# Two projection tiles computed as a fifth seven-product pair instead of singly, with one tile instead of two kept for the end of the input projection

## The chip, the cores and the metric

The kernel runs on one core of one Trainium2 chip. The metric is device time in microseconds (us) of that core; lower is better. The profile names five engines: PE (TensorE, with PEld for its weight loads), DVE (VectorE), ACT (ScalarE), POOL (GpSimd) and SP (SyncE, which here issues nearly all DMAs).

## The reference

One decoder layer over 1024 tokens with model width 1024, all in float32:

```python
u = rms_norm(x, norm1_g)
z = u @ w_in                      # 1024 x 3584: 28 tiles of 128 columns
y_conv = group_rms_norm(cb * causal_dwconv3(cc * ch, conv_w), conv_norm_g, 8)
o = chunkwise_retention(rotary(q), rotary(k), v)          # 4 heads x 128
y_ret = group_rms_norm(o, ret_norm_g, 4) * silu(rg)       # rg: tiles 20 to 23
x = x + concat(y_conv, y_ret) @ w_out
x = x + relu(rms_norm(x, norm2_g) @ w_up)**2 @ w_down
out = rms_norm(x, final_norm_g)
```

What matters here is the end of `u @ w_in`: its last tiles are the gates `rg`, one tile per retention head (tile 20 + h gates head h), and what follows, `concat(y_conv, y_ret) @ w_out`, which needs all eight tiles of y (four of the convolution, y0 to y3, and four of the heads, y4 to y7).

## The kernel before, in words

Everything is kept transposed: 128 channels by 1024 tokens make a tile, and the tokens are split into two halves of 512. Float32 products are done in three matmuls: each operand is split into a rounded high part and the rest (`wh` and `wl` for weights, `uh`/`ul`, `yh`/`yl` or the two halves of `U` for activations), and high times high, high times low and low times high are accumulated in a PSUM bank of 128 x 512 (`b`). A split is a cast on ACT and a subtraction on DVE or POOL. So one tile of the input projection over one half of the tokens is 8 blocks of 128 channels times 3 = 24 matmuls.

The tiles of the input projection are computed in one of three ways.

- `whole(f)` (L744, through `tile_in`, L520): one tile over both halves, 48 matmuls in four slots of 12. The results are read from PSUM by DVE.
- `pair_in((f, g))` (L824): two tiles at once by a Strassen-like scheme: seven products of 12 matmuls (`product`, L779) in the place of eight. It needs sums of the inputs (`U`, the four entries t1 to t4, 16 units of on-chip memory of 128 x 1024), sums of the weight blocks (four POOL subtractions or additions in `Left.split`, L209), seven weight splits, and DVE additions that put the products together in on-chip memory. The products come in the order `UP_ORDER`; of the second tile, half 1 is finished with product 7 and half 0 with product 4.
- the end (L910 to L926): the tiles of `IN_END` over half 0, then over half 1, each step 12 matmuls.

Before, the turns are 0, 1, 2, 3, 20, the pairs (4, 5), (6, 7), (8, 9), (10, 11), then tile 21 whole, then 22 and 23 by halves at the end: four slots for tile 21 and eight for the end.

On-chip memory is full at this place, so y0, y1 and the outputs of heads 2 and 3 are spilt to DRAM (`put_by`, L867) and fetched back (`get_back`, L876) on SP's queue. SP's queue also fetches the weight pieces (`r`, four buffers): a piece's DMA waits there until its buffer is free, and everything issued after it waits behind it. The split weights have four buffers too, so ACT can run at most four pieces ahead of PE.

After the end the first matrix of the next stage, `group(0)` (L1060), starts at once on PE: its first step multiplies the first `w_out` piece with half 0 of y0, y1, y2 and y3 in this order (`yh`, `yl`).

Between PE's products the kernel places the work of the other engines with a small planner: each conv, gate, norm or split is a generator, and `background` (L428) chooses, by a cost table of its own, which engine gets the next step and where in the program it stands. The program is static: each engine runs its list in order. `done` and `norm` (L471) are the group norm of a conv tile: a square on ACT, two matmuls on PE (L483, L484), a reciprocal root on ACT and three operations on DVE. `gate` (L719) multiplies with the token norm `R`, applies Silu on ACT and multiplies with the head's output on DVE. The reciprocal root and Silu each need a table load on ACT when they alternate.

Of the kernel before, what the change touches and what calls it, by code (L numbers as in the profile page):

```python
# [36 lines left out]


IN_QK = [12, 13, 16, 17, 14, 15, 18, 19]
IN_TURNS = [0, 1, 2, 3, 20, (4, 5), (6, 7), (8, 9), (10, 11), 21]  # L40
IN_END = [22, 23]
SLOT, LOOK, PE_MARGIN, LATE = 2.72, 3.2, 1.2, 0.0
WARM = 10
NORM_MARGIN, STEP_MARGIN, POOL_LATE = 6.5, 0.3, 1.0
# [35 lines left out]
def hybrid_layer(  # L80
# [18 lines left out]
    now, clock, procs, got = [0.0], {}, [], {}  # L99
# [24 lines left out]
    def unit(dt=F32, s="u"):  # L124
        return big.tile([P, T], dt, tag="u", name=nm(s))
# [6 lines left out]
    def bank(pool_=None):  # L132
        return (pool_ or pm).tile([P, H], F32, tag="b", name=nm("b"))
# [54 lines left out]
    IN_ORDER = list(IN_QK)  # L188
    for turn in IN_TURNS + IN_END:
        IN_ORDER += turn if isinstance(turn, tuple) else [turn]  # L190
# [37 lines left out]
    ahead = 3  # L228
    for turn in IN_TURNS + IN_END:
        if isinstance(turn, tuple):  # L230
            o = Left(mix, 1)
# [190 lines left out]
    def spawn(gen, ready=None, late=0.0):  # L422
        Task(gen, now[0] if ready is None else ready, late).go()
# [4 lines left out]
    def background(look=LOOK):  # L428
        while True:
            best = None  # L430
            for task in list(procs):
                want = task.want
                if want is None or isinstance(want, float):
                    if task.ready + (want or PE_MARGIN) <= now[0] or look > 1e6:
                        best = (-1.0, task, None)
                        break
                elif isinstance(want, tuple) and isinstance(want[0], Engine):
                    for eng in want:
                        start = max(clock[eng], task.ready)
                        if start < now[0] + look:  # L440
                            end = start + eng.cost(H) + task.late
                            if best is None or end < best[0]:
                                best = (end, task, eng)
                elif want in got:
                    best = (-1.0, task, got[want])
                    break
            if best is None:
                return
            _, task, eng = best
            if isinstance(eng, float):  # L450
                task.ready = max(task.ready, eng)
                task.go()
            elif eng is None:
                task.go()
            else:
                clock[eng] = max(clock[eng], task.ready)
                task.go(eng)
                task.ready = max(task.ready, clock[eng])
# [4 lines left out]
    def force(key):  # L463
        while key not in got:
            background(1e9)
            assert key in got, key

    y, y_h, y_l = [None] * KT, [None] * KT, [None] * KT
# [108 lines left out]
    o_n, retention_task = {}, [None, None]  # L577
# [166 lines left out]
    def whole(f):  # L744
        def evac(z):
            if f < 20 and f % 3 == 0:
                out = a_of[f // 3] = unit(s="a")
                for half, sl in enumerate(hs):
                    act.copy(out[:, sl], z[half])
                return  # L750
            out = None if f < 20 and f % 3 == 1 else unit(s="z")
            for half in range(2):
                spawn(use(f, half, out, z[half], True), clock[dve])

        tile_in(evac)
# [12 lines left out]
    U = {}  # L768
# [55 lines left out]
    def pair_in(fs):  # L824
        out = [unit(s="z") for _ in range(2)]
        (c11, c12), (acc, c22) = ([o[:, sl] for sl in hs] for o in out)
        for at, n in enumerate(UP_ORDER):
            if not got.get("pairs") and n in (5, 6, 7, 4):
                for j in range(4):
                    force(({5: "t1", 6: "t2", 7: "t3", 4: "t4"}[n], j))  # L830
            b = product(n, (pm, pr)[at % 2])
            slot()
            prepare()
            ready = None
            if n == 1:
                act.copy(acc, b)
            if n == 2:
                dve.tensor_add(c11, acc, b)
                ready = 0, 0
            if n == 5:  # L840
                b5 = b
            if n in (6, 7, 4):
                dve.tensor_add(acc, acc, b)
            if n == 6:
                dve.tensor_add(c12, acc, b5)
            if n == 7:
                dve.tensor_add(c22, acc, b5)
                ready = 1, 1
            if n == 3:
                dve.tensor_add(c12, c12, b)  # L850
                ready = 0, 1
            if n == 4:
                ready = 1, 0
            if ready:
                f, half, o = fs[ready[0]], ready[1], out[ready[0]]
                if f < 20 and f % 3 == 0:
                    a_of[f // 3] = o
                else:
                    spawn(use(f, half, o, o[:, hs[half]], False), clock[dve], LATE * half)
            tick()  # L860
        got["pairs"] = now[0]
# [5 lines left out]
    def put_by(key, of, *ready):  # L867
        for r in ready:
            yield r
        yield (dve,)  # L870
        t = of()
        spilt[key] = spill.tile([P, T], F32, tag="sp", name=nm("sp"))
        nc.sync.dma_start(spilt[key], t)
        mark(("by", key), dve)

    def get_back(key):  # L876
        t = unit(s="back")
        nc.sync.dma_start(t, spilt.pop(key))
        return t

    def split_y(idx, half):
        yield "y", idx, half
        if idx < 2:
            yield "back", idx
        yield (act,)
        split_y_hi(idx, half)
        eng = yield (pool, dve)
        split_y_lo(idx, half, eng)
        mark(("split", idx, half), eng)
# [3 lines left out]
    for i in range(2):  # L893
        spawn(put_by(("y", i), lambda i=i: y[i], ("y", i, 0), ("y", i, 1)))
    for at, turn in enumerate(IN_TURNS):
        if isinstance(turn, tuple):
            pair_in(turn)
        else:
            whole(turn)
        if at == len(IN_TURNS) - 2:  # L900
            for h in (2, 3):
                force(("by", ("o", h)))
                o_n[h, 0] = o_n[h, 1] = get_back(("o", h))
            for i in range(2):
                force(("by", ("y", i)))
                y[i] = get_back(("y", i))
                got["back", i] = now[0] + 10.0
    for idx in range(KT):
        spawn(split_y(idx, 0))
    ends = {f: (unit(s="z"), [bank() for _ in hs], []) for f in IN_END}  # L910
    for half in range(2):
# [547 lines left out]
    o = unit(s="end")  # L1459
# [104 lines left out]
```

## Time and profile before

| quantity | value |
|---|---|
| median of 3 runs | 1070.92 us (1070.82 to 1071.99) |
| the profiled execution's own time | 1070.03 us |
| its span, first to last instruction | 1068.1 us |
| time around the span | 1.93 us |
| PE busy | 1054.8 us (99% of the span) |
| DVE busy | 870.8 us (82%) |
| POOL busy | 561.6 us (53%) |
| ACT busy | 463.6 us (43%) |
| PE's granted clock | 0.999 of full speed |

How to read it: the profile is of one execution, whose own time lies 0.89 us below the median. In a timeline or a group of lines, a row names the engine, the line of the kernel, the operation, the tile written and the tiles read, with the shapes; "idle before" is the time the engine stood still ahead of it and what it then waited for. Nearly all operations outside PE are issued through one helper and carry its line, L74, so they are told apart by the names of their tiles: `wh`, `wl` weight splits; `yh`, `yl` splits of y; `r` weight pieces or the small tiles of a norm; `z` results of projection tiles; `cv` a convolution; `back` a tile fetched back; `q` the output of a head.

### The profile page before, as it was taken

The page shows a single profiled execution, that of the slowest core. Times are in us where ns is not written, and L with a number is a line of the kernel's source. Part 1 is how long each engine was busy: PE and PEld are TensorE (multiplying, and loading weights), DVE is VectorE, ACT ScalarE, POOL GpSimd, SP SyncE. Part 2 cuts the span into 40 slices and gives each one's busy share as a digit, 9 for nine tenths or more (in the row PEclk, how much of TensorE's full clock was granted, in tenths as well). Part 3 has the DMA queues.
Part 4 walks back from the last instruction along what each step waited for, and adds up shares of the span by engine and source line. Part 5 has one row for each costly group of instructions (what it writes and reads, how often), then busy time and mean ns, then how long its engine had stood idle before and what let it go on. Part 6 is the DMA issues. An engine that isn't in the chain of part 4 may idle for free.

```text
span 1068.1 us, 13853 instructions
## 1 busy us (share of the span) xinstructions
PE 1054.8 (99%) x4860; PEld 879.2 (82%) x4860; DVE 870.8 (82%) x1231; ACT 463.6 (43%) x906; POOL 561.6 (53%) x381
## 2 busy tenths in 40 slices
PE   9999999999999999999999999999999999999997
PEld 8888888788888888788788888888888888888886
DVE  7446546799998665799999989999899899899955
ACT  8211445673437444443343433343443434334453
POOL 6334324367854233559458267277186295384552
PEclk9999999999999999999999999999999999999999
DMA  7121122122223733051221211211301201200204
GB/s 276 65 58 42 38 80 70 63 95 80 69 69 129 256 115 123 11 187 39 61 59 49 79 31 50 90 30 50 99 21 50 89 21 49 90 21 19 69 30 158
DMA packets 39685, 82.25 MB, mean 77 GB/s; under 512 B 4544, under 2 KB 5696, under 8 KB 39616
## 3 DMA queue, kind: packets, MB, share of 16 engines
q1 hardware_dynamic: 39328, 80.85, 23.5%
q8 instruction: 38, 0.62, 0.2%
q10 hardware_dynamic: 288, 0.52, 0.1%
q14 instruction: 31, 0.25, 0.1%
HBM read 71.92 MB, written 9.44 MB: 76 GB/s over the span
## 4 chain that ended last, share of the span: by engine, by line
PE 90%; DVE 6%; ACT 2%; issue 1%; POOL 1%; DVEq 0%; ACTq 0%; POOLq 0%
PE b L403 55%; PE b L1277 23%; PE b L357 4%; PE b L1386 4%; DVE t L74 1%; DVE wl L74 1%; DVE x L74 1%; DVE m L74 1%; ACT h L74 1%; DVE q L74 1%; DVE V L74 1%; PE b L339 0%; PE b L595 0%; PE b L1436 0%; PE b L246 0%
## 5 line engine op out<-in xcount | busy, mean ns | idle before, releaser
L74 ACT CAST wh<-r 128x512 fp32r<-128x512 f32 x286 | 176.6, 620 | 326.4 <-PE b L403 134.4
L403 PE MATMUL b<-U,wh 128*128 128x512 f32 x1024 | 315.8, 390 | 2.0 <-DVE x L74 1.2
L74 DVE TENSOR_TENSOR wl<-r,wh 128x512 fp32r<-128x512 f32 x250 | 232.8, 933 | 89.0 <-ACT wh L74 87.8
L74 POOL TENSOR_TENSOR r<-r,r 128x512 f32<-128x512 f32 x136 | 210.2, 1548 | 114.1 <-DVE wl L74 66.1
L1277 PE MATMUL b<-V,wh 128*128 128x512 f32 x784 | 242.0, 389 | 0.7 <-POOL V L74 0.4
L403 PEld LDWEIGHTS b<-U,wh 128*128 128x128 f32 x1024 | 191.7, 188 | 43.2 <-issue 2.4
L74 DVE TENSOR_TENSOR x<-x,b 128x512 f32<-128x512 f32 (+1 forms) x312 | 195.5, 673 | 28.8 <-PE b L1386 14.3
L403 PE MATMUL b<-U,wl 128*128 128x512 f32 x512 | 199.2, 389 | 0.0
L1277 PEld LDWEIGHTS b<-V,wh 128*128 128x128 f32 x784 | 147.1, 188 | 32.4 <-POOL V L74 0.9
L74 POOL TENSOR_TENSOR t<-t,t 128x512 f32<-128x512 f32 x70 | 106.3, 1523 | 96.4 <-ACT t L74 50.4
L1277 PE MATMUL b<-V,wl 128*128 128x512 f32 x392 | 152.5, 389 | 0.0
L74 POOL TENSOR_TENSOR wl<-r,wh 128x512 fp32r<-128x512 f32 x36 | 51.4, 1432 | 119.3 <-ACT wh L74 116.5
L403 PEld LDWEIGHTS b<-U,wl 128*128 128x128 f32 x512 | 96.1, 188 | 19.9
L403 PE MATMUL b<-uh,wh 128*128 128x512 f32 x304 | 102.3, 396 | 0.0
L403 PE MATMUL b<-ul,wh 128*128 128x512 f32 x304 | 100.5, 390 | 0.0
L403 PE MATMUL b<-uh,wl 128*128 128x512 f32 x304 | 100.2, 389 | 0.0
L1277 PEld LDWEIGHTS b<-V,wl 128*128 128x128 f32 x392 | 73.6, 188 | 15.2
L74 POOL TENSOR_TENSOR V<-t,V 128x512 fp32r<-128x512 f32 x35 | 49.6, 1418 | 67.0 <-ACT V L74 67.0
L74 DVE TENSOR_TENSOR t<-t,b 128x512 f32<-128x512 f32 x112 | 75.8, 677 | 1.7 <-POOL t L74 1.2
L74 ACT ACTIVATE t<-t 128x512 f32<-128x512 f32 x64 | 40.2, 631 | 81.2 <-DVE t L74 80.5
L74 DVE TENSOR_TENSOR V<-t,V 128x512 fp32r<-128x512 f32 x63 | 70.3, 1116 | 0.0
L403 PEld LDWEIGHTS b<-uh,wl 128*128 128x128 f32 x304 | 57.0, 188 | 12.3
(177 smaller groups left out, 1431.3 us busy)
## 6 DMA issues: line engine op xcount, KB each, us to landing
r<-w_up_t SPq DMA_DIRECT2D x64, 256.0 KB, 2.6
r<-w_down_t SPq DMA_DIRECT2D x56, 256.0 KB, 2.7
r<-w_in_t SPq DMA_DIRECT2D x48, 256.0 KB, 2.7
xt<-xT SPq DMA_DIRECT2D x16, 256.0 KB, 5.4
xs<-xT SPq DMA_DIRECT2D x8, 512.0 KB, 5.0
r<-w_out_t SPq DMA_DIRECT2D x16, 256.0 KB, 2.7
x<-xT SPq DMA_DIRECT2D x8, 512.0 KB, 7.9
k<-x SPq DMA_DIRECT2D x6, 512.0 KB, 3.0
```

What stands on the lines that cost most here:

```text
L74: return f(out, *args, **kw)
L357: nc.tensor.matmul(vb[i], a[k][:, i * P : (i + 1) * P], b[k // 2][:, vs], start=(k == 0 and a is uh and b is vh), stop=(k == KT - 1 and a ...
L403: nc.tensor.matmul(b, a[:, k, :], rhs(n, k)[r], start=(start and i == 0), stop=(stop and i == len(ops) - 1),)
L1277: nc.tensor.matmul(b, a, r, start=(i == 0), stop=(i == len(ops) - 1))
L1386: nc.tensor.matmul(z, a, b, start=(k == 0 and t == 0), stop=(k == 3 and t == 2))
```

## The change

Tiles 21 and 22 become a fifth pair, the last of the turns, and only tile 23 is left for the end. The outputs of heads 2 and 3 are fetched back ahead of that pair, y0 and y1 only behind it: the input sums `U` are given up there, and their memory takes the two tiles.

```diff
-IN_TURNS = [0, 1, 2, 3, 20, (4, 5), (6, 7), (8, 9), (10, 11), 21]
-IN_END = [22, 23]
+IN_TURNS = [0, 1, 2, 3, 20, (4, 5), (6, 7), (8, 9), (10, 11), (21, 22)]
+IN_END = [23]
...
     for at, turn in enumerate(IN_TURNS):
+        if at == len(IN_TURNS) - 1:
+            for h in (2, 3):
+                force(("by", ("o", h)))
+                o_n[h, 0] = o_n[h, 1] = get_back(("o", h))
         if isinstance(turn, tuple):
             pair_in(turn)
         else:
             whole(turn)
-        if at == len(IN_TURNS) - 2:
-            for h in (2, 3):
-                force(("by", ("o", h)))
-                o_n[h, 0] = o_n[h, 1] = get_back(("o", h))
-            for i in range(2):
-                force(("by", ("y", i)))
-                y[i] = get_back(("y", i))
-                got["back", i] = now[0] + 10.0
+    U.clear()
+    for i in range(2):
+        force(("by", ("y", i)))
+        y[i] = get_back(("y", i))
+        got["back", i] = now[0] + 6.0
```

The planner then lays out the other engines' lists anew from pair (10, 11) on. Three places matter for what follows.

**ACT, from the Silu of a gate to the split of y0, half 0.** Before, with `back_2887` for y0, `back_2889` for y1, and `r_2993`, `r_3029` for the two norms of conv tile y3:

```order
L74 ACT_TABLE_LOAD
L74 ACTIVATE z_2965<-z_2965 128x512 x2
L74 ACT_TABLE_LOAD
L74 ACTIVATE r_2993<-b_2990,eps 128x512
L74 ACTIVATE r_2994<-r_2993 128x512
L74 CAST yh_2997<-back_2887 128x512
L74 CAST yh_3001<-back_2889 128x512
L74 CAST yh_3005<-z_2535 128x512
L74 CAST yh_3010<-q_617 128x512
L74 ACTIVATE r_3029<-b_3026,eps 128x512
L74 ACTIVATE r_3030<-r_3029 128x512
L74 CAST yh_3035<-q_618 128x512
```

In the changed kernel, with `back_3059` for y0, `r_3051` and `r_3081` for the same two norms and `z_2881` for the gate of tile 22:

```order
L74 ACT_TABLE_LOAD
L74 ACTIVATE r_3051<-b_3048,eps 128x512
L74 ACTIVATE r_3052<-r_3051 128x512
L74 ACT_TABLE_LOAD
L74 ACTIVATE z_2881<-z_2881 128x512
L74 ACT_TABLE_LOAD
L74 ACTIVATE r_3081<-b_3078,eps 128x512
L74 ACTIVATE r_3082<-r_3081 128x512
L74 CAST yh_3087<-z_2535 128x512
L74 CAST yh_3091<-z_2702 128x512
L74 CAST yh_3095<-q_617 128x512
L74 CAST yh_3113<-back_3059 128x512
```

The cast of y0 moved from behind the first norm to behind both norms, one more Silu, three table loads and three other casts.

**DVE, from the convolution of y3's second half to the gate of tile 21.** Before, `z_2965` is the gate of tile 21, read straight from PSUM:

```order
L74 SCALAR_TENSOR_TENSOR cv_2777<-z_2536,sm,cv_2777 128x512 x2
L74 TENSOR_TENSOR wl_2876<-r_2775,wh_2875 128x512
L74 TENSOR_TENSOR z_2702<-z_2702,b_2860 128x512
L74 TENSOR_TENSOR z_2702<-z_2702,R 128x512
L74 TENSOR_TENSOR z_2702<-z_2702,cv_2777 128x512
L74 TENSOR_TENSOR wl_2928<-r_2795,wh_2927 128x512
L74 TENSOR_TENSOR s_2933<-t_2911,s_2912 128x512
L74 TENSOR_TENSOR z_2965<-b_2891,R 128x512
L74 TENSOR_TENSOR z_2965<-b_2892,R 128x512
L74 SCALAR_TENSOR_TENSOR q_618<-z_2965,sm,q_618 128x512 x2
```

In the changed kernel the same gate is `z_2880`, put together from the products `b_2905`, `b_2959`, `b_2932`, `b_2982`, with `z_2881` as the running sum:

```order
L74 SCALAR_TENSOR_TENSOR cv_2777<-z_2536,sm,cv_2777 128x512 x2
L74 TENSOR_TENSOR wl_2919<-r_2744,wh_2918 128x512
L74 TENSOR_TENSOR z_2880<-z_2881,b_2905 128x512
L74 TENSOR_TENSOR z_2880<-z_2880,R 128x512
L74 TENSOR_TENSOR wl_2946<-r_2775,wh_2945 128x512
L74 TENSOR_TENSOR s_2954<-t_2928,s_2929 128x512
L74 SCALAR_TENSOR_TENSOR q_618<-z_2880,sm,q_618 128x512
L74 TENSOR_TENSOR z_2881<-z_2881,b_2959 128x512
L74 TENSOR_TENSOR z_2880<-z_2881,b_2932 128x512
L74 TENSOR_TENSOR wl_2998<-r_2899,wh_2997 128x512
L74 TENSOR_TENSOR z_2880<-z_2880,b_2982 128x512
L74 TENSOR_TENSOR z_2880<-z_2880,R 128x512
```

The last row, the gate of tile 21 over half 1, now stands behind the sums of five products and four weight splits; the two multiplications of `z_2702` with `R` and `cv` went to POOL.

**SP, around the fetches from the spill.** `sp_1993` and `sp_1995` are the heads' outputs, `sp_2223` and `sp_2584` are y0 and y1. Before:

```order
L162 DMA r_2849<-w_out_t 128x512
L162 DMA r_2873<-w_out_t 128x512
L878 DMA back_2883<-sp_1993 128x1024
L878 DMA back_2885<-sp_1995 128x1024
L878 DMA back_2887<-sp_2223 128x1024
L878 DMA back_2889<-sp_2584 128x1024
L162 DMA r_2925<-w_out_t 128x512
L162 DMA r_2959<-w_out_t 128x512
```

In the changed kernel:

```order
L878 DMA back_2876<-sp_1993 128x1024
L878 DMA back_2878<-sp_1995 128x1024
L162 DMA r_2899<-w_in_t 128x512
L162 DMA r_2922<-w_out_t 128x512
L162 DMA r_2949<-w_out_t 128x512
L162 DMA r_2972<-w_out_t 128x512
L162 DMA r_2995<-w_out_t 128x512
L162 DMA r_3017<-w_out_t 128x512
L162 DMA r_3041<-w_out_t 128x512
L878 DMA back_3059<-sp_2223 128x1024
L878 DMA back_3061<-sp_2584 128x1024
```

The fetches of y0 and y1 moved behind seven weight pieces, each of which waits in the queue until its buffer is free. On PE, the 96 matmuls of tiles 21 and 22 become seven products of 12; the rest keeps its count.

## The prediction

> **What bounds the kernel now.** I read the page first, then the waits of PE, the chain that ended last around the change, and the busy time of 20 us stretches.
>
> ```profile
> PE 1054.8 (99%) x4860; PEld 879.2 (82%) x4860; DVE 870.8 (82%) x1231; ACT 463.6 (43%) x906; POOL 561.6 (53%) x381
> PE b L663 <- ACT h L74: 2.3, 5, 0.7
> PE b L246 <- DVE t L74: 1.1, 1, 1.1
> 328.81 51.23 PE b L403 x226
> 305.00:325.00 20.00, 20.00 (x90) 16.56 (x89) 19.00 (x23) 8.30 (x15) 9.51 (x7) 1.00 0.39 121
> 325.00:345.00 20.00, 20.00 (x90) 16.54 (x89) 16.11 (x20) 14.91 (x24) 9.73 (x8) 1.00 0.24 84
> 302.81 0.39 PE L403 MATMUL b<-uh,wh 128*128 128x512 f32 x1
> 344.97 0.39 PE L403 MATMUL b<-yh,wh 128*128 128x512 f32 x1
> ```
>
> PE is the bound. Its largest waits are the two shown (2.3 us in all, no single one over 1.1), and the chain around the change is nothing but matmuls: 226 in 51.23 us, 0.2267 us each. But DVE is busy for 19.00 of the 20 us ahead of the end of the projection, so PE has its data only because these were made early. I take 302.81 (product 3 of pair (10, 11)) as the common start: up to there both kernels run the same lists. The first matmul of the output projection starts at 344.97, 186 matmuls later.
>
> **What is saved.** Tiles 21 and 22 cost 96 matmuls as wholes and 84 as a pair, so PE would reach the output projection 12 x 0.2267 = 2.72 us earlier: 302.81 + 174 x 0.2267 = 342.25. That is 0.25% of the kernel, just above the 0.2% (2.14 us) that a measurement can tell from no change. The profiled execution took 1070.03 us (span 1068.1 and 1.93 around it), the median is 1070.92. Every difference below is worked out against the profiled execution and added to the median.
>
> **What is added and what covers it.** The pair brings four POOL sums of weights, three more weight splits, and six more DVE operations (seven sums, less one multiplication that goes to POOL). They run beside PE and cost nothing by themselves, if DVE, ACT and POOL are not late. These rows tell how late they are.
>
> ```profile
> 309.07 2.19 DVE L74 TENSOR_TENSOR z<-z,b 128x512 f32<-128x512 f32 x3
> 311.90 0.69 DVE L74 SCALAR_TENSOR_TENSOR b<-b,r 128x512 f32<-128x512 f32 x1
> 312.51 1.40 DVE L74 SCALAR_TENSOR_TENSOR z<-z,less_g,r 128x512 f32<-128x512 f32 x1
> 322.66 1.36 DVE L74 TENSOR_TENSOR wl<-r,wh 128x512 fp32r<-128x512 f32 x1 [0.59 <-ACT wh L74]
> 326.31 1.42 DVE L74 SCALAR_TENSOR_TENSOR q<-z,sm,q 128x512 f32<-128x512 f32 x2 [0.49 <-ACT z L74]
> ```
>
> The first of the three sums at 309.07 takes product 6, whose last matmul started at 302.58: DVE is some 6 us behind. Before, that did no harm: y0's cast for the output projection ran at 329.37, 15.6 us ahead of its use.
>
> **The chain to the output projection.** In the changed kernel's lists the gate of tile 21 over half 1 (the last row of the second DVE list above) is the 22nd DVE operation from 311.90 on. Their durations:
>
> ```profile
> L74 DVE TENSOR_TENSOR wl<-r,wh 128x512 fp32r<-128x512 f32 x8 | 9.2, 1153 | 0.8 <-ACT wh L74 0.6
> L74 DVE TENSOR_TENSOR z<-z,b 128x512 f32<-128x512 f32 x13 | 8.8, 681 | 0.2
> L74 DVE SCALAR_TENSOR_TENSOR cv<-z,sm,cv 128x512 f32<-128x512 f32 x2 | 2.4, 1204 | 0.0
> L74 DVE TENSOR_TENSOR s<-t,s 128x512 fp32r<-128x512 f32 x2 | 1.6, 796 | 1.6 <-ACT s L74 1.6
> L74 DVE TENSOR_TENSOR z<-z,R 128x512 f32<-128x512 f32 x1 | 1.1, 1074 | 0.0
> L74 POOL TENSOR_TENSOR r<-r,r 128x512 f32<-128x512 f32 x4 | 6.2, 1571 | 0.2
> L74 POOL TENSOR_TENSOR wl<-r,wh 128x512 fp32r<-128x512 f32 x9 | 12.9, 1456 | 10.8 <-ACT wh L74 10.8
> L74 POOL TENSOR_TENSOR z<-z,R 128x512 f32<-128x512 f32 x2 | 3.5, 1734 | 3.4 <-DVE z L74 3.4
> ```
>
> Nine of the 22 read a PSUM bank: 9 x 0.68 = 6.1. The others are six weight splits (6 x 1.15), two of `cv` (2.4), two with `R` (2.15), the norm's second step (1.4), one `s` (0.8) and one `q` (0.71): 14.4. Neighbours overlap by some 0.07 (311.90 to 312.51 is 0.61 for a row of 0.69), 1.5 in all, so 19.0 us. DVE waits twice for ACT on the way, which I put at the 0.59 and 0.49 shown. The gate is through at 311.9 + 19.0 + 1.1 = 332.0. The four POOL sums (4 x 1.57 = 6.3 us) lie beside this. From there the engines hand the work to and fro, and ACT's rows tell the rest:
>
> ```profile
> 324.35 1.28 ACT L74 ACT_TABLE_LOAD   x1
> 325.64 1.16 ACT L74 ACTIVATE z<-z 128x512 f32<-128x512 f32 x2
> 326.82 1.28 ACT L74 ACT_TABLE_LOAD   x1
> 328.11 0.69 ACT L74 ACTIVATE r<-b,eps 128x512 f32<-128x512 f32 x1
> 328.83 0.63 ACT L74 ACTIVATE r<-r 128x512 f32<-128x512 f32 x1
> 329.37 0.60 ACT L74 CAST yh<-back 128x512 fp32r<-128x512 f32 x1
> 330.17 0.62 ACT L74 CAST yh<-back 128x512 fp32r<-128x512 f32 x1 [0.20 <-DMA back<-sp]
> 330.70 0.62 ACT L74 CAST yh<-z 128x512 fp32r<-128x512 f32 x1
> ```
>
> After 332.0: Silu of tile 21 (0.6) and the cast of a `w_out` piece (0.6), to 333.2; POOL's split of that piece (1.46) and, behind it in POOL's list, the gate of tile 22 times `R` (1.73), to 336.4; its Silu and the next cast (1.1), to 337.5; then on ACT without a gap the first list of the change: a table load (1.29 from start to start), the two steps of a norm (1.26 from start to start), a load, Silu (0.6), a load, two steps, to 344.5; three casts of 0.53, and y0's cast, to 346.7. PE is there at 342.25, so its first matmul waits 4.4 us. Before it goes on it needs y0's low part, which DVE makes after the second norm's three steps, tile 23's gate and a head's product: 344.5 and six operations of 0.6 to 0.75, 348.5. The fifth matmul needs y1's low part, POOL's third split after 345.1: 345.1 + 3 x 1.46 = 349.5. The eight matmuls left take 1.8, so the step ends at 351.3. Before, it ended at 344.97 + 2.72 = 347.69. **The sum is +3.6 us**: a stall of 6.3 less the 2.7 saved.
>
> Two things lie just beneath. SP issues y0's fetch behind a weight piece whose buffer is freed by a DVE split at about 338.
>
> ```profile
> DMA to landing us min/median/max: 3.6/7.5/8.7
> k<-x SPq DMA_DIRECT2D x6, 512.0 KB, 3.0
> ```
>
> At 338.5 + 7.5 (the fetches of before) it lands at 346.0, just ahead of its cast at 346.1; with 3.6 (or 3.0, as another fetch of this size) at 342, with 8.7 it adds 1.1. So were ACT faster, the fetch would be late next. And within the pair the weights have little to spare: `wl_2919` for product 7 is due at 325.5 and made at about 324.5, a stall of up to 0.5 that disappears in the later one. What follows (heads' splits, first sums of the output projection) has at least the steps of the first group, 2.72 us each, in hand; I cost it at nothing.
>
> **Bounds.** Below: the gate of tile 21 cannot pass before product 3 is done (302.81 + 98 x 0.2267 = 325.0, 0.39 for the last) and two DVE operations of 0.68, so 326.8 in the place of 332.0: 3.6 - 5.2 = -1.6. Above: DVE's splits beside POOL take up to 1.77 against 1.15, and POOL is busier now; half of the 13 operations at 0.6 more adds 4, +7.6. I take 332.0, since the means are of the stretch ahead of it, where POOL was as busy.
>
> ```profile
> 284.61 1.77 DVE L74 TENSOR_TENSOR wl<-r,wh 128x512 fp32r<-128x512 f32 x1
> 1.05 4.22 PE L246 MATMUL b<-t 128*128 128x128 f32 x20 [1.05 <-DVE t L74]
> 1055.06 1.05 PE L1440 MATMUL b<-ident,x 128*128 128x128 f32 x8
> 1055.95 0.73 PE L313 MATMUL b<-ones,ssq 128*128 128x1 f32 x6
> ```
>
> PE's clock is the other unknown. At the trace's start, after standing still, PE took 4.22 us for 20 rows of a small matmul, 0.21 each; at 1055.06 eight such rows took 0.89, 0.11 each. If the stall slows PE in the same way, some 4.2 us run at half pace and 2.1 us are lost: +5.7. The trace has no wait of this length later, so it cannot say; I leave it out of the sum and keep it in the range. The Trainium skill ("TensorE: Matmul & The Clock Gate", Part 1: The HAM clock gate) states that an idle window of about 3.4 us halves the clock until about 3.4 us of work have gone by; by that figure I estimate a loss of 1.7 us and +5.3 in the place of +3.6.
>
> A table load takes 1.29 us here until the next operation starts (324.35 to 325.64). The Trainium skill ("ScalarE: Activation LUTs", What ACT_TABLE_LOAD costs) adds 1.38 us of drain to each switch; by that estimate the three loads would make the sum +7.7. The row decides.
>
> **The rivals.**
> 1. *The slack holds; faster.* If DVE catches up (it has 16.1 of 20 us from 325 on) and y0 is ready by 342.25, the 2.72 us are kept: 1068.2. It decides at the gate of tile 21: it would have to be through by 327, and the hand-offs behind it 1 us shorter as well. Against it: product 3 alone ends at 325.4. Chance 0.09.
> 2. *A stall that only eats the gain.* The gate at 327 to 330.5: within 2.1 us of before, about 1071. For it: the rows at 0.68 when POOL rests. Chance 0.24.
> 3. *The stall also slows PE's clock*, as at the start: +5.7, 1076.6. For it: PE does one matmul in over 6 us. Against it: the profile's granted clock never falls. Chance 0.20. The section of the skill on the clock gate, named above, is the rule for it.
> 4. *A longer chain:* the fetch of y0 at 8.7 or DVE's splits at 1.77, +4.7 to +7.6: up to 1078.5. Chance 0.03.
> 5. *Table loads hold ACT for longer than their row*, by one more load each: 3 x 1.28 = 3.8, so +7.4, 1078.3. Against it: 0.01 us between the load's end and the next operation. Chance 0.02. It is what the skill's section on the table load states.
> 6. *The change doesn't do what it says:* excluded, PE's list has the seven products.
>
> **How the numbers follow.** The forecast itself, a stall of 5 to 8 us and +2.2 to +5.1, has 0.42. The time is 1070.92 + 3.6 = 1074.5. Slower by over 0.2%: 0.42 + 0.20 + 0.03 + 0.02 = 0.67; within: 0.24; faster: 0.09. The range runs from 1069.5 (the lower bound of -1.6, rounded) to 1078.5 (+7.6), which leaves out the full gain and what goes beyond 4.
>
> **What would show it.** In the profile of the changed kernel: one PE wait of 4 to 5 us ahead of `b<-yh`, put down to ACT, with a second of about 2 us behind it; three table loads on ACT between the gate of tile 22 and the first `yh`; the first group's first step ending 3 to 4 us later than 347.7. If PE starts on `yh` at 342.3 without a wait, the chain is wrong; if the waits are there and the matmuls behind them are further apart than 0.23 us, the clock is the missing term; if the cast waits for `back<-sp`, the fetch was the bound.

## The result and the profile after

| | median | ratio to before, 95% interval |
|---|---|---|
| before | 1070.97 us (1070.82 to 1071.99, 4 runs) | |
| after | 1082.37 us (1082.13 to 1082.69, 4 runs) | 1.0105, 1.0093 to 1.0117 |

The change makes the kernel slower by 11.4 us, where 3.6 were forecast: the direction was right, the size was outside the range of 1069.5 to 1078.5. The profiled execution took 1082.69 us, its span is 1080.6, 12.5 more than the 1068.1 of before; single executions scatter by a microsecond or two around the medians.

The page of the changed kernel, its busy times and its granted clock in 40 slices of 27 us:

```profile
PE 1055.8 (98%) x4848; PEld 878.4 (81%) x4848; DVE 876.8 (81%) x1241; ACT 468.2 (43%) x912; POOL 567.4 (53%) x385
...
PEclk9999999999998899999999999999999999999999
```

PE has its 12 matmuls less (4848 for 4860) and is busy 1.0 us longer all the same: in two slices the clock is not full. Now the waits of PE (us in total, times, the longest):

```profile
PE b L403 <- ACT yh L74: 5.8, 1, 5.8
PE b L403 <- DVE yl L74: 4.1, 1, 4.1
...
PE b L403 <- DVE t L74: 1.1, 1, 1.1
```

Two waits are new and long, both at the start of the output projection. Before, the longest single one was 1.1 us. Here they are on PE's timeline, with the first matmuls behind them:

```profile
342.27 0.39 PE L403 MATMUL b<-uh,wl 128*128 128x512 f32 x1
348.47 0.79 PE L403 MATMUL b<-yh,wh 128*128 128x512 f32 x1 [5.82 <-ACT yh L74]
353.38 0.79 PE L403 MATMUL b<-yl,wh 128*128 128x512 f32 x1 [4.12 <-DVE yl L74]
353.98 0.63 PE L403 MATMUL b<-yh,wl 128*128 128x512 f32 x1
354.40 0.63 PE L403 MATMUL b<-yh,wh 128*128 128x512 f32 x1
...
358.24 0.63 PE L403 MATMUL b<-yh,wh 128*128 128x512 f32 x1
358.67 0.52 PE L403 MATMUL b<-yl,wh 128*128 128x512 f32 x1
359.03 0.39 PE L403 MATMUL b<-yh,wl 128*128 128x512 f32 x1
```

The last matmul of the input projection starts at 342.27, and the next one only 6.2 us later. That is one lone matmul, then PE waits again. From 353.98 on the matmuls are 0.42 to 0.43 us apart, and from 359.03 on 0.23. The step's twelve matmuls are over when the thirteenth starts, at 358.24. Before, that was at 347.69:

```profile
347.69 0.39 PE L403 MATMUL b<-yh,wh 128*128 128x512 f32 x1
```

So 10.55 us of the loss stand in this one step. The two matmuls behind it, still slow, lose 0.34 more, and 1.6 of the 12.5 come later.

The busy time of PE, PEld, DVE, ACT and POOL in stretches of 5 us, then the granted clock, the DMA share and GB/s:

```profile
345.00:350.00 5.00, 0.79 (x1) 0.29 (x1) 3.58 (x5) 4.95 (x9) 3.07 (x3) 0.53 0.02 10
350.00:355.00 5.00, 1.61 (x4) 1.33 (x5) 5.00 (x5) 3.05 (x5) 4.46 (x3) 0.50 0.00 0
355.00:360.00 5.00, 5.00 (x16) 3.91 (x15) 4.96 (x10) 3.12 (x6) 0.00 (x0) 0.61 0.72 238
360.00:365.00 5.00, 5.00 (x24) 4.12 (x23) 4.37 (x8) 2.30 (x5) 0.00 (x0) 1.00 1.01 365
```

The clock falls while PE stands still and is at half for nearly four more microseconds of the third stretch, in which PE works without a pause: 16 matmuls in the place of the 24 of the fourth.

What PE waits for, on ACT first:

```profile
339.10 1.28 ACT L74 ACT_TABLE_LOAD   x1
340.39 0.69 ACT L74 ACTIVATE r<-b,eps 128x512 f32<-128x512 f32 x1
...
345.72 0.63 ACT L74 ACTIVATE r<-r 128x512 f32<-128x512 f32 x1
346.26 1.12 ACT L74 CAST yh<-z 128x512 fp32r<-128x512 f32 x2
...
347.80 1.13 ACT L74 CAST yh<-back 128x512 fp32r<-128x512 f32 x2
```

The order is the one forecast: the loads and the two norms, three casts, then y0's cast, which is through at about 348.4 (the first of the two in the last row). No row has a wait for a DMA, so y0's fetch is not the bound. On DVE, from the gate of tile 21 on:

```profile
332.59 1.08 DVE L74 TENSOR_TENSOR z<-z,R 128x512 f32<-128x512 f32 x1
...
346.38 0.70 DVE L74 SCALAR_TENSOR_TENSOR b<-b,r 128x512 f32<-128x512 f32 x1 [2.52 <-ACT r L74]
346.99 1.76 DVE L74 SCALAR_TENSOR_TENSOR z<-z,less_g,r 128x512 f32<-128x512 f32 x1
348.78 0.69 DVE L74 SCALAR_TENSOR_TENSOR z<-b,z 128x512 f32<-128x512 f32 x1
349.39 0.68 DVE L74 TENSOR_TENSOR z<-b,R 128x512 f32<-128x512 f32 x1
349.99 1.67 DVE L74 SCALAR_TENSOR_TENSOR back<-z,sm,back 128x512 f32<-128x512 f32 x1
351.58 1.75 DVE L74 TENSOR_TENSOR yl<-back,yh 128x512 fp32r<-128x512 f32 x1
```

And on POOL in the same time:

```profile
346.93 2.95 POOL L74 TENSOR_TENSOR yl<-z,yh 128x512 fp32r<-128x512 f32 x2 [9.03 <-ACT yh L74]
349.85 1.26 POOL L74 TENSOR_TENSOR yl<-back,yh 128x512 fp32r<-128x512 f32 x1
351.07 1.71 POOL L74 TENSOR_TENSOR yl<-q,yh 128x512 fp32r<-128x512 f32 x1
```

These are the six DVE operations ahead of PE's second matmul, the last of them y0's low part. I had put them at 0.6 to 0.75 each; they take 6.95 us together. The ones that read a PSUM bank (`b`) keep their 0.68 to 0.70. The three with both inputs in SBUF, the on-chip memory outside PSUM, take 1.67 to 1.76. All six lie beside POOL's low parts. A few microseconds earlier, at 340.32 and 342.39, the same kernel has two operations of the same kinds (`back<-z,sm,back` and `z<-z,less_g,r`) while POOL stands idle, and they take 0.74 us each.

### The profile page after: what moved, and what is told of

Same layout as the page of the kernel before. It is cut to its first block, busy times and chain, and to the rows that moved or that the text cites. A ratio compares the mean times of both kernels' runs of the same rounds, so it can differ in the third digit from the quotient of the medians.

```text
span 1080.6 us, 13854 instructions
## 1 busy us (share of the span) xinstructions
PE 1055.8 (98%) x4848; PEld 878.4 (81%) x4848; DVE 876.8 (81%) x1241; ACT 468.2 (43%) x912; POOL 567.4 (53%) x385
## 4 chain that ended last, share of the span: by engine, by line
PE 59%; DVE 4%; POOL 2%; issue 1%; DMA 1%; ACT 0%; DVEq 0%; POOLq 0%
PE b L403 32%; PE b L1278 22%; PE b L1387 4%; DVE wl L74 1%; DVE x L74 1%; DMA x<-k 1%; DVE t L74 1%; POOL r L74 1%; POOL x L74 1%; DVE V L74 0%; PE b L1437 0%; POOL t L74 0%; DVE out L74 0%; PE b L313 0%; POOL V L74 0%
## 5 line engine op out<-in xcount | busy, mean ns | idle before, releaser
L403 PE MATMUL b<-U,wh 128*128 128x512 f32 x1056 | 325.7, 390 | 3.0 <-DVE x L74 1.2
L74 DVE TENSOR_TENSOR wl<-r,wh 128x512 fp32r<-128x512 f32 x255 | 237.8, 934 | 96.7 <-ACT wh L74 94.3
L74 POOL TENSOR_TENSOR r<-r,r 128x512 f32<-128x512 f32 x140 | 216.1, 1546 | 114.6 <-DVE wl L74 66.4
L403 PEld LDWEIGHTS b<-U,wh 128*128 128x128 f32 x1056 | 197.7, 188 | 45.4 <-issue 1.9
L403 PE MATMUL b<-U,wl 128*128 128x512 f32 x528 | 205.5, 389 | 0.0
L403 PEld LDWEIGHTS b<-U,wl 128*128 128x128 f32 x528 | 99.2, 188 | 20.7
L403 PE MATMUL b<-uh,wh 128*128 128x512 f32 x284 | 95.8, 397 | 0.0
L403 PE MATMUL b<-ul,wh 128*128 128x512 f32 x284 | 94.0, 390 | 0.0
L403 PE MATMUL b<-uh,wl 128*128 128x512 f32 x284 | 93.8, 390 | 0.0
L403 PEld LDWEIGHTS b<-uh,wl 128*128 128x128 f32 x284 | 53.3, 188 | 11.9 <-POOL wl L74 0.4
```

The lines of the kernel that those rows point to most:

```text
L74: return f(out, *args, **kw)
L403: nc.tensor.matmul(b, a[:, k, :], rhs(n, k)[r], start=(start and i == 0), stop=(stop and i == len(ops) - 1),)
```

## The experiments

My theory after this comparison: the pair's results come too late by as much as forecast and a little more (first wait). POOL's low parts then stretch DVE's (second wait), and the pause halves PE's clock. The rivals: the late fetch of y0, or the shorter end by itself, and not the pair; table loads that cost more than their rows; and a pair that takes from DVE and ACT what it saves on PE. Each diff is against the changed kernel, if nothing else is said.

### The fetch earlier

```diff
-            pair_in(turn)
+            pair_in(turn, fetch_y if at == len(IN_TURNS) - 1 else None)
```

Here `fetch_y`, called after the last pair's product 5, gives up the sums t1 and fetches y0 and y1 into their place.

> The changed kernel, with y0 and y1 fetched back right behind product 5 of the last pair (about 12 us earlier on SP's queue); the other engines' lists nearly keep their order: y0's cast on ACT moves ahead of three others, y2's low part takes the place of y0's in DVE's list. Theory (the place of the splits in the lists of ACT and DVE sets the stall): the first wait of PE shrinks from 5.8 to about 4.3 us, but the next one, now for y2's low part, still ends near 353, so 1080 to 1082 us. Rival (the late fetch from the spill sets it): with y0 landed some 10 us ahead of its use the waits go, below 1074.

Measured: 1080.13 us, ratio 1.0081 (1.0061 to 1.0100). SP's queue and PE's waits in this kernel:

```profile
327.54 0.86 SPq L880 DMA_DIRECT2D back<-sp  x2
```

```profile
PE b L403 <- ACT yh L74: 4.3, 1, 4.3
...
PE b L403 <- DVE yl L74: 1.8, 1, 1.8
```

The fetch is issued 12.7 us earlier than at 340.26 in the changed kernel, and the stall stays. The 2.2 us gained against the changed kernel probably come from the other order that ACT's and POOL's lists take; I did not test that. With y0 there in time the stall is still there, so the late fetch is not the cause.

### The fetch and all splits earlier

To the above is added that the splits of y are queued at that same place instead of behind the pair, so that ACT casts each tile as soon as it is there:

```diff
+        for idx in range(KT):
+            spawn(split_y(idx, 0))
...
-    for idx in range(KT):
-        spawn(split_y(idx, 0))
```

> As the early fetch, and the splits of all eight y tiles over half 0 are offered to the planner at that place too, so that ACT casts y2, both heads' tiles, y0 and y1 ahead of the two norms of y3 and of the table loads. Theory: PE waits only for y3's low part, about 0 to 2 us, its clock stays up, and the 2.72 us saved come through: 1068.5 to 1071. Rival (the pair's own extra work on DVE, or the pair as such, is what costs): the waits stay, over 1076.

Measured: 1070.45 us, ratio 0.9993 (0.9983 to 1.0002). Its one new wait in this stretch, and the stretch's busy times and clock:

```profile
PE b L403 <- POOL yl L74: 0.9, 1, 0.9
```

```profile
340.00:345.00 5.00, 5.00 (x23) 4.13 (x22) 4.96 (x6) 4.86 (x7) 5.00 (x4) 1.00 0.22 67
345.00:350.00 5.00, 4.07 (x18) 3.06 (x17) 5.00 (x7) 4.19 (x6) 4.23 (x4) 1.00 0.10 40
```

The whole stall was a matter of order: y0's cast stood behind the loads and norms. With it in front, and the fetch early enough for that, the clock stays at 1.00 and the kernel is level with before. Of the 2.72 us saved nothing clear of noise shows in the medians. In the profile 1.2 us are left: from the common start (302.81 before, 305.70 here) to the end of the first step (347.69 and 349.41) PE takes 43.7 us in the place of 44.9. The execution profiled here had lost 2.9 us ahead of that start, all of it ahead of its hundredth matmul, where both kernels run the same list. DVE, ACT and POOL are busy for nearly all of the 10 us shown, and the next late thing is y3's low part.

### No table loads

The gates apply Square in the place of Silu. Their values are other ones, but ACT no longer alternates between two tables:

```diff
-        act.activation(g[:, sl], g[:, sl], AF.Silu)
+        act.activation(g[:, sl], g[:, sl], AF.Square)
```

> The changed kernel with Square in the place of Silu in the gates, so that the gates' values are other ones and ACT's table loads around them go; lists otherwise in the same order. Theory (ACT's chain of three loads, two norms and a Silu stands between the gate and y0's split): three loads of 1.29 go, y0's cast and DVE's operations behind the second norm move up by some 3.9 us: 1077 to 1079, to 1075 if PE's clock then stays up. Rival (DVE behind POOL's splits, or the fetch, is what is late): 1081 or more.

Measured: 1077.49 us, ratio 1.0057 (1.0042 to 1.0072). PE's waits:

```profile
PE b L403 <- DVE yl L74: 4.1, 1, 4.1
...
PE b L403 <- ACT yh L74: 2.2, 1, 2.2
```

The first wait falls by 3.6 us. That is close to three loads of 1.29, but it is not their sum: a fourth load, ahead of tile 21's first Silu (at 326.42 in the changed kernel), is gone too, and ACT now waits 1.37 us for DVE once (ahead of tile 22's second Silu, at 341.24). The time was met in part by luck. What a load costs is better read in the changed kernel's rows above: ACT's next operation starts at 340.39, 0.01 us behind the end of the load at 339.10, so no further cost of a load stands there. The second wait stays at 4.1 us, so its length does not hang on the loads.

### Work for PE in the pause

44 matmuls whose result nobody reads stand between the two projections (0.2267 x 44 = 10.0 us):

```diff
+    idle = bank(pr)
+    for _ in range(DUMMIES):
+        nc.tensor.matmul(idle, uh[7][:, :P], uh[7][:, hs[1]], start=True, stop=True)
```

> The changed kernel, with 44 more matmuls (10 us) on PE that nobody reads, put ahead of the output projection, where PE stands still for 10 us. Theory (the stall also halves PE's granted clock, and 14 matmuls behind it run at half pace): the clock stays up, the waits end where they did, 2.5 to 3 us less: 1079.2 to 1080. Rival (the slow matmuls wait for their data, not for the clock): no change, 1082.4, or slower if the new matmuls come late.

Measured: 1078.55 us, ratio 1.0070 (1.0055 to 1.0085). PE's second matmul on y, and the clock:

```profile
354.45 0.50 PE L403 MATMUL b<-yl,wh 128*128 128x512 f32 x1 [0.65 <-DVE yl L74]
```

```profile
350.00:355.00 5.00, 4.35 (x19) 3.30 (x18) 5.00 (x5) 4.01 (x6) 5.00 (x4) 1.00 0.00 0
```

The second wait is down to 0.65 us, since the useless work lasts nearly until y0's low part is there, and the clock is 1.00. By the medians the kernel is 3.8 us faster than the changed one, though PE does 10 us more of work. So the halved clock is a cost of its own. By the changed kernel's timeline it is 2.70 us: thirteen matmuls take 5.65 us (353.38 to 359.03) in the place of 2.95. Counted from the common start (302.75 there, 303.64 here), PE is 2.4 us ahead at the fifteenth matmul on y (359.03 there, 357.54 here), and its wait at the start of the MLP is 0.4 us shorter. The rest of the 3.8 lies within the intervals of the two ratios.

### Half as much work in the pause

The same with 20 matmuls (4.5 us), so that most of the first wait is filled and the second is left.

> The changed kernel with 20 matmuls whose result nobody reads in the first wait, instead of 44: 4.5 us of work, to about 347, so that PE stands still for about 1.5 us ahead of the first yh and then 4 to 5 us ahead of the second. Theory (a pause of about 3 us is what halves the clock, and one matmul in between counts for little): the clock is halved in the second wait and for the matmuls after it, and only the first part of the loss goes: 1080.5 to 1082.5. Rival (only the long first pause does it): the clock stays at 1.00, as with 44, and the time is 1078 to 1079.5.

Measured: 1081.9 us, ratio 1.0103 (1.0089 to 1.0116). On PE:

```profile
349.50 0.50 PE L403 MATMUL b<-yh,wh 128*128 128x512 f32 x1 [1.30 <-ACT yh L74]
354.42 0.80 PE L403 MATMUL b<-yl,wh 128*128 128x512 f32 x1 [4.42 <-DVE yl L74]
...
357.15 0.49 PE L403 MATMUL b<-yl,wh 128*128 128x512 f32 x1
357.48 0.39 PE L403 MATMUL b<-yh,wl 128*128 128x512 f32 x1
```

```profile
350.00:355.00 5.00, 0.58 (x2) 0.50 (x2) 5.00 (x5) 4.06 (x6) 5.00 (x4) 0.55 0.00 0
```

The first pause is down to 1.3 us and the clock is halved all the same, for 2.7 us of work (354.42 to 357.15) instead of 5.3. So the rival fell. The theory was not right either. A mean clock of 0.55 means half rate for 4.5 of these 5 us, so the clock fell at about 350.5, only 0.5 us into the second wait (350.00 to 354.42). In the 3.4 us ahead of that, PE had stood still for 1.8 in all, 1.3 of the first wait and 0.5 of the second. Two pauses with one lone matmul between them count together. That the first wait of 5.8 us is enough by itself shows in the next run.

### The low parts on DVE alone

```diff
-        eng = yield (pool, dve)
+        eng = yield ((pool, dve) if half else (dve,))
```

This is in `split_y`: POOL makes no low part of half 0, and so lies idle beside DVE's six operations.

> The changed kernel with the low parts of half 0 of y all made by DVE, so that POOL makes no split beside DVE's six operations ahead of y0's low part. Theory (those six take 6.95 us instead of 4.0 because POOL works on the same memory beside them): they take about 4 us, PE's second wait falls from 4.1 to 1 to 1.5 us, and the time to 1078.5 to 1080; the clock is still halved after the first wait. Rival (the six are slow by themselves, or held by their reads of PSUM): the second wait stays near 4 us, 1082 or more, since the low parts of y1 to y3 then queue on DVE as well.

Measured: 1078.88 us, ratio 1.0073 (1.0059 to 1.0087). PE's waits, and DVE's six operations:

```profile
PE b L403 <- ACT yh L74: 5.8, 1, 5.8
...
PE b L403 <- DVE yl L74: 1.1, 1, 1.1
```

```profile
347.63 0.74 DVE L74 SCALAR_TENSOR_TENSOR z<-z,less_g,r 128x512 f32<-128x512 f32 x1
...
349.61 0.74 DVE L74 SCALAR_TENSOR_TENSOR back<-z,sm,back 128x512 f32<-128x512 f32 x1
350.27 1.29 DVE L74 TENSOR_TENSOR yl<-back,yh 128x512 fp32r<-128x512 f32 x2
```

DVE makes five low parts more here, and y0's comes earlier. The same two operations that took 1.76 and 1.67 us take 0.74, y0's low part 0.65, and the six together some 3.9 instead of 6.95: the first starts 0.61 ahead of the first row shown, at 347.02, and y0's low part ends at 350.9. The second wait loses these 3.0 us, the kernel 3.5. That DVE's operations were slow because POOL worked beside them is shown. The clock still falls: its mean is 0.81 from 345 to 350, so it is at half from about 348.1, ahead of PE's first matmul on y at 349.11.

### Two single tiles instead of the pair

```diff
-IN_TURNS = [0, 1, 2, 3, 20, (4, 5), (6, 7), (8, 9), (10, 11), (21, 22)]
+IN_TURNS = [0, 1, 2, 3, 20, (4, 5), (6, 7), (8, 9), (10, 11), 21, 22]
```

The heads' outputs are fetched ahead of 21, as ahead of the pair; y0 and y1 still behind 22.

> The pair is undone: tiles 21 and 22 are single turns, and only tile 23 is left for the end; y0 and y1 are still fetched late, between tiles 22 and 23. PE has the 96 matmuls of before for the three tiles. Theory (the pair's late results cause the stall: its last two products, the two gates and a norm all come in the last 7 us): the gates of 21 and 22 are through earlier, a wait of 0 to 3 us is left ahead of the first yh, for the norm and the cast of y0 behind tile 23's Silu, and the time is 1071 to 1074. Rival (leaving one tile for the end with the late fetch is enough for the stall, whatever 21 and 22 are): a first wait of 4 us or more, the clock halved, 1077 or more.

Measured: 1071.61 us, ratio 1.0007 (0.9998 to 1.0016). PE's first matmul on y:

```profile
345.03 0.39 PE L403 MATMUL b<-yh,wh 128*128 128x512 f32 x1
```

There is no wait ahead of y at all. One tile at the end does no harm by itself, nor does a fetch behind the last turn (issued at 336.29, 4.0 us earlier than in the changed kernel); the pair just ahead of them, with its lists as they are laid out, does. At 498.07, at the start of the MLP, PE waits 0.65 us for a DVE operation, which before doesn't have. It does so here without any stall, so this much of what comes later probably belongs to the order of the lists behind the projection.

### Early splits with y0 to y3 on DVE

Against the kernel with early splits, `split_y` gives the low parts of y0 to y3 to DVE.

> The early fetch and early splits (1070.45 on another call), with the low parts of y0 to y3 on DVE instead of the engine that the planner chooses; POOL's split of y3, which PE waited 0.94 us for, goes to DVE. Theory (that wait is all that keeps the kernel from the gain here): about 0.9 us less than the kernel with early splits, 1069 to 1070, a ratio to the kernel before of 0.998 to 0.999. Rival (DVE, busy for 4.9 of each 5 us there, is the bound, and the work only moves): the wait is put down to DVE, no gain, a ratio of 0.999 to 1.001.

Measured: 1071.51 us, ratio 1.0006 (0.9997 to 1.0015). In place of POOL's 0.9 PE now waits

```profile
PE b L403 <- DVE yl L74: 1.6, 1, 1.6
```

so the rival held: DVE is full, and the work only moves.

### A fifth pair with eight steps left

The single tile 20 goes into a pair with 21, and 22 and 23 stay for the end, in three orders. The first:

```diff
+IN_TURNS = [0, 1, 2, 3, (4, 5), (6, 7), (8, 9), (10, 11), (20, 21)]
+IN_END = [22, 23]
```

> A fifth pair with two tiles left for the end: the single tile 20 is dropped, (20, 21) is the fifth pair, behind (10, 11), and 22 and 23 go by halves at the end as before, so that the pair's results have eight steps of 2.72 us, 21.8 us, before the output projection instead of four. The same 12 matmuls are saved. Theory (the pair itself is worth its 2.72 us, and only the short end takes it away): no wait of PE ahead of yh, 1067.6 to 1069.2, a ratio of 0.997 to 0.9985. Rival (the single tile 20 is needed ahead of the first pair, whose input sums U are last written at 239.5 in the profile of before: the first pair now starts 10.9 us earlier and waits for them): a wait ahead of a product of the first pair takes the gain or more, 1070 or more.

> The same with (20, 21) as the fourth of five pairs, and (10, 11), whose norms are the longest chain to y3, as the last. Theory: eight steps are enough for the norms too, as the same as behind the other order, 1067.6 to 1069.5. Rival (the norms of (10, 11) need the time of more than eight steps, as they had twelve in the kernel before): a wait ahead of yl or yh of y3, 1070 or more.

> The same with (20, 21) as the first of the five pairs. Theory (the place among the pairs does not matter as long as eight steps are left): as the two others, 1067.6 to 1069.5. Rival (its gates need the heads' outputs and stay queued, or the first pair waits for U): a wait in the first pair or behind it, 1070 or more.

Measured, in this order: 1083.26 us, ratio 1.0114 (1.0100 to 1.0128); 1087.9, 1.0148 (1.0134 to 1.0162); 1088.1, 1.0155 (1.0141 to 1.0169). The waits of the first and of the second:

```profile
PE b L403 <- ACT U L74: 9.2, 1, 9.2
```

```profile
PE b L403 <- ACT yh L74: 2.9, 1, 2.9
```

In all three the first pair waits some 9 us for its input sums: tile 20 was the cover for them. The rival held. That takes more than the gain, and so the worth of the pair alone stays unmeasured. Beside it two things can be read. With (20, 21) last, no wait ahead of yh is left, so eight steps were enough for a pair of gates there. With (10, 11) last, 2.9 us are left, and 3.0 in the third order, ahead of y3's cast: eight steps were not enough for the two norms of y3. All three had stood still early on, so the other engines may have had more time than they would have without that.

### Another order of the products

Against the kernel with early splits, the order of a pair's products is changed:

```diff
-UP_ORDER, MLP_ORDER = (1, 2, 5, 6, 3, 7, 4), (1, 2, 6, 5, 3, 7, 4)
+UP_ORDER, MLP_ORDER = (1, 2, 5, 6, 7, 4, 3), (1, 2, 6, 5, 3, 7, 4)
```

Product 3 then takes its weights from a buffer that already holds a later piece, so the pairs' sums are not those of the reference.

> The kernel with early fetch and early splits (1070.45), and in every pair the products in the order 1 2 5 6 7 4 3 instead of 1 2 5 6 3 7 4, so that the half 0 of the second tile, which the output projection needs first, is done one product earlier and the half 1 of the first tile last. Theory (what is left of the loss is the end of DVE's queue ahead of y3's low part; a product less behind half 0 shortens it): the wait of 0.9 us ahead of yl goes, 1069 to 1070. Rival (DVE is full from 335 to 352 and POOL's work beside it stretches its operations, so the order of the products changes nothing): 1070 to 1071.5, with a wait of 0.5 to 2 us left.

Measured: 1076.32 us, ratio 1.0044 (1.0031 to 1.0058). The two longest of its new waits:

```profile
PE b L403 <- ACT yh L74: 1.6, 1, 1.6
...
PE b L403 <- POOL wl L74: 0.9, 1, 0.9
```

Neither side had it: the order moves other things to the front too, and new waits come up. Why, I did not follow; with the other buffers the run is inconclusive on the order. One thing can be read. Its waits at the start of the output projection (0.9, 0.7 and 1.6 us within 5 us) are short, and yet the clock falls: it is 0.50 from 355 to 360. In the kernel with y0 to y3 on DVE a single wait of 1.6 us left it at full rate.

No kernel here beats the one before. The kernel with early splits is level with it.

## Why the prediction was right in direction and wrong in size

**The 2.72 us saved** hold but for 0.25: the projection's last matmul starts at 342.27, 0.23 before the 342.5 at which PE could have gone on; 342.25 was forecast.

**The gate of tile 21** is through at 333.67 instead of 332.0. The 19.0 us for DVE's list were enough: its 22 operations took 18.2 from 312.08 on, waits left out. What was too small is the 1.1 us of waits on the way. DVE waited 3.4 us, 1.32 for POOL (at 318.90), 1.25 and 0.83 for ACT (at 324.32 and 328.37); the wait for POOL was not in the sum at all. This delay stays: the first table load starts at 339.10 instead of 337.5, and y0's cast lets PE's first matmul start at 348.47 instead of 346.7 (+1.77).

**The hand-offs and ACT's chain** hold to within 0.2 us, three table loads by their rows among them. The fetch was no bound, as the sum had it.

**The step that failed** is "344.5 and six operations of 0.6 to 0.75, 348.5". From y0's cast to PE's second matmul I had 1.8 us; it took 4.91 (+3.11). The same paragraph put three POOL low parts into exactly these microseconds, and I had a row at 1.77 us for a DVE split beside POOL, but used it only as a bound on the earlier chain. The run with the low parts on DVE shows the cause. The Trainium skill ("SBUF — State Buffer", Who interferes with whom) states that a DVE instruction with two inputs in SBUF contends with a GpSimd instruction that reads SBUF, and one with at most one SBUF input, outside DVE's two-port modes, does not. The rows agree: 1.67 to 1.76 us for the first kind, 0.68 to 0.70 for the second, beside the same POOL work.

**The clock** was left out of the sum, "I leave it out of the sum and keep it in the range". From the second matmul to the step's end I had 2.8 us, 0.3 of it a wait for y1's low part that did not come; it took 358.24 - 353.38 = 4.86 (+2.06). Rival 3 had the mechanism and 2.1 us for it. Both runs with added matmuls show it. The "granted clock never falls" of before was no evidence against it: before had no pause to make it fall.

**What follows, "I cost it at nothing"**, costs 12.5 - 10.55 = 1.9 us in the profile. The last of the slow matmuls are 0.34 of it, a wait of 1.1 us at the start of the MLP is most of the rest; the run with two single tiles has 0.65 of such a wait without any stall. Some 0.5 stays open.

Together: 3.6 + 1.77 + 3.11 + 2.06 = 10.54, the 10.55 that the step's end is late. **The rivals were not alternatives.** A longer chain (rival 4) and the slower clock (rival 3) came together, each of about the size given, though the chain grew mostly at the six DVE operations and not at the splits that I had in mind; my range took the larger of them where it should have taken their sum. Even that sum (+9.7, 1080.6) would have stayed short of the 1082.37 measured. Rival 1 fell with the gate of tile 21, rival 2 with both waits, rival 5 with ACT's rows, in which nothing stands between a load and the next operation. That the stall needs the pair with its lists as laid out here, not the late fetch or the single tile at the end, the runs on these show; the kernel with early splits has the pair and no stall. One reading of before was off without any effect: PE's second largest wait was 1.2 us for DVE, in two parts of at most 0.7.

## What to carry to other kernels

A pair of products that saves work delivers its results late, so ask what stands in the consumer's way behind it; here the order of ACT's list, not the amount of work, made 11 us of loss or none. When PE is forecast to stand still for about half of a stretch of 3.4 us, in one wait or in several, put the slower clock into the sum at once (here 1.8 us of standing still in such a stretch lowered it), and add costs that can come together before setting the range. And price each DVE operation by its operands and by what POOL does in the same microseconds, not by its mean.

## What the runs showed of the hardware that I had not expected

The clock's half-rate stretch outlasts the pause. In the changed kernel the matmuls are back at 0.23 us from 359.03 on, 5.65 us after they go on at 353.38. With 20 added matmuls they are at 357.48, 3.1 us after they go on at 354.42. A lone matmul in the pause (348.47) does not bring the clock back. In the trace's record of the granted clock the half-rate stretches last 13.65 us (changed kernel), 10.24 (no table loads) and 6.83 (20 added matmuls, and low parts on DVE): four, three and two times 3.41. The Trainium skill ("TensorE: Matmul & The Clock Gate", Part 1: The HAM clock gate) states a free-running window of about 3.4 us, and that an idle window halves the clock. The lengths agree: the slow stretch comes in whole windows. That the window must be idle did not hold here. By PE's rows, the windows at whose end the clock fell at the start of the output projection held PE work for 0% of their length (early fetch, and low parts on DVE), 23% (changed kernel), 35% (no table loads), 42% (the other order of the products) and 47% (20 added matmuls), while one of 60% (low parts on DVE, 341.2 to 344.7) left it at full rate. So short waits close together can halve the clock: those of 0.7 and 1.6 us with the other order of the products did, where a single one of 1.6 us with y0 to y3 on DVE did not. My estimates of 1.7 and 2.1 us were a little too small for the 2.70 lost in the changed kernel.

Two engines at work together can be slower than one alone: when DVE took over POOL's low parts of half 0, y0's let PE go on 1.9 us after its first matmul on y (349.11 to 351.01) instead of 4.9.
